# Moving three accumulating weight-sum transfers from a mixer to the feed-forward behind it, and one weight load behind a statistics exchange

## The chip, the cores and the metric

One core of one Trainium2 chip runs the whole program in one launch. The metric is device time in microseconds (us), the median of several runs. Engines are named as in the profile: PE is TensorE, PEld its weight loads, DVE is VectorE, ACT is ScalarE, POOL is GpSimd, SP is SyncE, which here only issues DMAs. An engine's name with a q (SPq) is its queue of instructions.

## The reference

A decoder trunk of two layers on x of shape (1, 512, 1024) in float32. Each layer is a mixer and a gated feed-forward, both between RMS norms and added to the residual:

```
for i in range(2):
    h = rms_norm(x, pre_g);  h = mixer_i(h);  x = x + rms_norm(h, post_g)
    h = conv_ffn(rms_norm(x, ffn_pre_g[i]), w_up[i], conv_w[i], conv_b[i], w_down[i])
    x = x + rms_norm(h, ffn_post_g[i])

def conv_ffn(h, w_up, conv_w, conv_b, w_down):        # 1024 -> 2 x 2816 -> 1024
    u = causal_dwconv(h @ w_up, conv_w, conv_b)       # width 3
    gate, up = split(u, 2);  return (silu(gate) * up) @ w_down
```

The change lies in layer 1. Its mixer projects h to queries, keys and values of three groups of dilated sliding-window attention (group 0 with window 128 and step 1, groups 1 and 2 with steps 4 and 16), whose outputs are merged by the groups' softmax denominators, and of a stick-breaking attention; the concatenated outputs go through one output projection.

## The kernel before, in words

**Products.** Every float32 product is made of three float32r matmuls. A weight block W is loaded raw and split: ACT casts it to a high part (line 84, tile wh), DVE subtracts that to get a low part (line 85, wl). The class `Weights` does this for a list of units in order. `load()` (line 55) takes one of three raw buffers of the tag wraw (128 x 1024) and has SP issue the DMA; `next()` hands out the next split unit and splits ahead by `depth` units. `W` holds nearly all weights of the program; `W2` holds two blocks of the mixer's output weights (od_w_out 0 and 1), split into space that other tiles have left.

**Sums of weights.** The feed-forward's up projection is made, for pairs of blocks 4 to 19, in a scheme of seven block products for eight (Strassen's with Winograd's sums). It needs sums of quarter blocks of the weights. These are not computed by an engine: POOL issues DMAs from DRAM to DRAM, some of which add to their destination (`accum_op`), into four tiles ws per group of pairs ("chunk": three pairs in chunks 0 to 3, two in chunks 4 and 5, as `CHUNKS` says). `sum_steps` (line 148) lists the eight moves of every chunk, step by step and in each step chunk by chunk:

```
steps = [(0, 3, bypass), (2, 2, bypass), (0, 2, add), (2, 0, add), (1, None, bypass),
         (1, 0, add), (3, -1, bypass), (3, 1, add)]          # (tile, source quarter or sum, how)
moves = [lambda c=c, step=step: move(c, *step) for step in steps for c in chunks]
```

The last step adds quarter 1 into tile 3. With a `mark` the list begins with a 4-byte DMA that reads a value of the program, so that the moves start no earlier than that value is there. `make_sums(layer, chunks, mark, left)` issues the moves on POOL but for the last `left`, which it returns.

For layer 1 this happens in three places: chunks 0 to 3 in the mixer from line 1627 (one mark and 32 moves), chunk 4 at the mixer's end (lines 1920, 1931 and 1977) and chunk 5, "its own" (`OWN`), at the begin of the feed-forward (line 405). SP reads the sums as weights (line 60, wraw<-ws), four blocks of 128 x 512 for each pair, the block of tile 3 last, among three blocks that come straight from the input.

**The mixer's end.** The code between line 1878 and line 1945 has its order written out by hand for PE, DVE, ACT, POOL and SP (`manual_schedule`): what stands first is issued first on each engine. A loop of four projections (n = 0 to 3, queries and keys of group 0) goes with the scores and softmaxes of groups 1 and 2 (`score12`, line 1740; `softmax12`, lines 1753 and 1757). `W2.next()` loads and splits od_w_out 0 behind n = 1, and `W2.load()` loads od_w_out 1 behind n = 2. Then:

```
exchange(1, st12)                # SP: write groups 1 and 2's maxima and sums to DRAM (stat)
project = proj_V()               # takes the four split blocks of the values' weights
tile_V(3, "a")                   # PE: values of 128 tokens; ACT copies; SP stores 4 x 64 KB (vst, cv)
exchange_back(1, on)             # SP: read them back in the other order of tokens (on)
for ...: score0(i, banks)        # PE, DVE, ACT: scores and softmaxes of group 0 (lines 1771 to 1780)
exchange(0, st0); tile_V(2, "s"); exchange_back(0, by_r)
W.load(); W.load()
share(st0, on, 0, ...)           # DVE: group 0's share of the merge; needs on (lines 1786 to 1794)
... scale0 (1820); wo2.append(W2.next())   # splits od_w_out 1
```

Then follow two more tiles of values, the other groups' share and scaling (line 1849), the transposes on PE (lines 1830 and 1859), the product with the values (line 1811) and the output projection (tile ao). A DMA that SP may not issue yet, since its buffer or its data aren't there, holds up those behind it on SP.

**The feed-forward's begin.** `ffn` (line 392) has POOL issue a spacer and its own chunk's moves. PE makes four blocks by plain products (u4), then two plain pairs, then the sixteen pairs by seven products (`seven`), whose order is written out by hand for PE, DVE and ACT.

Of the kernel before, what the change touches and what calls it, by code (L numbers as in the profile page):

```python
# [42 lines left out]
OWN = (5,), (5,)  # L43
# [55 lines left out]
def trunk(tc, A, out):  # L99
# [3 lines left out]
    with ExitStack() as top:  # L103
# [7 lines left out]
        def spacer(pool, w):  # L111

            POOL.memset(pool.tile([P, w], F32, tag="spacer", name="spacer", bufs=1)[:, 0:1], 0.0)
# [18 lines left out]
        lead = cst.tile([P, 72], F32, tag="lead", name="lead")  # L132
# [15 lines left out]
        def sum_steps(layer, chunks, mark=None, copies_first=False):  # L148

            wide = "(a q) c -> a (q c)"  # L150
            if layer not in sums_of:
                sums_of[layer] = [[dpool.tile([n * P, S], F32, tag=f"ws{layer}{j}{c}", name="ws")
                                   for c, n in enumerate(CHUNKS[layer])] for j in range(4)]
            tiles = sums_of[layer]

            def move(c, j, src, op):
                if src is None:
                    src = tiles[0][c][:]
                elif src < 0:
                    src = tiles[1][c][:]  # L160
                else:
                    at = sum(CHUNKS[layer][:c]) * P
                    src = A[f"ffn_up_q{layer}"][src, at:at + CHUNKS[layer][c] * P]
                nc.gpsimd.dma_start(tiles[j][c][:].rearrange(wide, q=4), src.rearrange(wide, q=4), accum_op=op,  # L164
                                    max_dma_last_dim=8192)

            steps = [(0, 3, ALU.bypass), (2, 2, ALU.bypass), (0, 2, ALU.add), (2, 0, ALU.add), (1, None, ALU.bypass),
                     (1, 0, ALU.add), (3, -1, ALU.bypass), (3, 1, ALU.add)]
            if copies_first:
                steps[4:] = [(1, 0, ALU.bypass), (3, 1, ALU.bypass), (1, None, ALU.add), (3, -1, ALU.add)]  # L170
            moves = [lambda c=c, step=step: move(c, *step) for step in steps for c in chunks]
            if mark is not None:
                moves.insert(0, lambda: nc.gpsimd.dma_start(tiles[0][chunks[0]][0:1, 0:1], mark))
            return moves

        def make_sums(layer, chunks, mark, left=0):
            moves = sum_steps(layer, chunks, mark)
            with tc.manual_schedule(engines={POOL.engine}):
                while len(moves) > left:
                    moves.pop(0)()  # L180
            return moves
# [20 lines left out]
                    up += [(A["ffn_w_up"][layer, f, z], 1024) for z in range(2)]  # L202
            return (up + [lambda n=n: down[layer](n) for n in range(4 * HF)])

        down, last_rstd = {}, {}
        units = []
        units += [(A["ev_w_c"][u], 832) for u in range(4)]
        units += [(A["ev_w_dqk"][0, 0], 1024), (A["ev_w_dqk"][0, 1], 1024)]
# [183 lines left out]
        def ffn(layer, xnT, pending, final):  # L392
            with ExitStack() as es:
# [8 lines left out]
                                  fp.tile([P, 1024], F32R, tag="gl", name="gl", bufs=HF))  # L402
                with tc.manual_schedule(engines={POOL.engine}):
                    spacer(fp, 80)
                    for move in sum_steps(layer, OWN[layer], last_rstd[layer][0:1, 0:1]) if OWN[layer] else ():
                        move()
                spill = tc_dram[layer]
                t2 = {}
# [1132 lines left out]
        def odd(xnT, pending, order):  # L1541
            xh, xl = xnT
            with ExitStack() as es:
# [44 lines left out]
                def proj_T(*args):  # L1588
                    for _ in T_parts(*args):
                        pass  # L1590
# [33 lines left out]
                DVE.tensor_copy(tri[:], trif[:])  # L1624

                ACT.copy(lead[0:1, 1:2], sv[0:1, 0, 0:1])
                make_sums(1, range(4), lead[0:1, 1:2])


                for u in range(2):  # L1630
# [98 lines left out]
                def score12(hp):  # L1729

                    zps = [[bank(t, "z12", 2, 2, P) for t in tags] for tags in ("ss", "tn")]
                    for rp, zp in enumerate(zps):
                        for rr in range(2):
                            r = 2 * rp + rr
                            c = slice(r * P, (r + 1) * P)
                            for g in range(2):
                                u = 2 * (g + 1) + hp
                                for y in range(2):
                                    rw = slice(y * 64, y * 64 + 64)
                                    PE.matmul(zp[y][:, rr, g], cq[u][rw, c], ck[u][rw, c], start=True, stop=True)  # L1740
                    return [lambda rp=rp, zp=zp: softmax12(hp, rp, zp) for rp, zp in enumerate(zps)]
# [56 lines left out]
                def exchange(n, src):  # L1798

                    d = dpool.tile([S, 8], F32, tag=f"stat{n}", name="stat")  # L1800
                    v = views[n] = [d[:].rearrange("(i q) c -> q i c", i=NT), d[:].rearrange("(q r) c -> q r c", r=4)]
                    nc.sync.dma_start(v[n], src[:].rearrange("p a b c -> p a (b c)"))

                def exchange_back(n, dst):
                    nc.sync.dma_start(dst[:].rearrange("p a b c -> p a (b c)"), views[n][1 - n])
# [68 lines left out]
                W2 = Weights(nc, None, [(A["od_w_out"][k], 1024) for k in range(2)], 2, wpool)  # L1874
# [5 lines left out]
                with tc.manual_schedule(engines={PE.engine, DVE.engine, ACT.engine, POOL.engine, nc.sync.engine}):  # L1880
                    for n, (x, t) in enumerate((x, t) for x in range(2) for t in (cq, ck)):
                        proj_T(t[x], (-0.125, 1.0)[t is ck], False, t is cq)
                        if n % 2 == 0:
                            softmaxes = score12(n // 2)
                        softmaxes.pop(0)()
                        if n == 1:
                            wo2.append(W2.next())
                        if n == 2:
                            W2.load()
                    exchange(1, st12)  # L1890
                    depth, W.depth = W.depth, 0
                    project = proj_V()

                    def tile_V(i, tag):
                        a = project(i, tag=tag)
                        st = chp.tile([P, 512], F32, tag="s", name="vst")
                        ACT.copy(st[:], a)
                        for r in range(4):
                            nc.sync.dma_start(cv12[32 * i:32 * i + 32, r], st[r::4, :])

                    tile_V(3, "a")
                    exchange_back(1, on)
                    for i, banks in zip((3, 2, 1, 0), ("ss", "tn", "aa", "oa")):
                        score0(i, banks)
                    exchange(0, st0)
                    tile_V(2, "s")
                    exchange_back(0, by_r)
                    W.load()
                    W.load()
                    share(st0, on, 0, slice(0, 4))  # L1910
                    for i in ORDER[:2]:
                        scale0(i)
                    wo2.append(W2.next())
                    tile_V(1, "s")
                    for i in ORDER[2:]:
                        scale0(i)
                    share(st12, by_r, 1, slice(0, 4))
                    tile_V(0, "a")

                    moves = sum_steps(1, (4,), shares[1][0:1, 0, 0:1], True)  # L1920
                    halves = [glob.tile([P, 2, 4, 256], F32, tag=tag, name="pt") for tag in ("xh", "xl")]
                    turned_to += [spare[:, 0], spare[:, 1]]
                    turned_to += [sb.tile([P, 4, 256], F32, tag=tag, name="pt")[:] for tag in ("sl", "sh")]
                    turned_to += [x[:, n] for x in halves for n in range(2)]
                    fours = [(hp, rp) for hp in range(2) for rp in range(2)]
                    pts = []
                    for n, i in enumerate(ORDER):
                        pts.append(turn0(i)())
                        scale12(*fours[n])
                        for _ in range((3, 1, 1, 1)[n]):  # L1930
                            moves.pop(0)()
                    for a in fours:
                        pts.append(turn12(*a)())
                    W.ahead(W.pos + 2)
                    oT = [bank("os"[k], "oT") for k in range(2)]
                    oG = [[ap.tile([P, S], F32R, tag=f"{t}{k}", name="og") for k in range(2)] for t in ("cq", "ck")]
                    for u in range(2):
                        for value, pt in zip([value0(i) for i in ORDER] + [value12(*a) for a in fours], pts):
                            value(pt, u)
                        split(oG[0][u][:], oG[1][u][:], oT[u])  # L1940
# [48 lines left out]

        xnT = even()  # L1990
        xnT = ffn(0, *xnT, False)
        xnT = odd(*xnT)
        ffn(1, *xnT, True)


# [99 lines left out]
```

## Time and profile before

| what | value |
|---|---|
| median of 3 runs | 1098.04 us (1097.97 to 1098.35) |
| profiled execution: its time | 1096.47 us |
| profiled execution: its span | 1094.7 us |
| granted PE clock | 0.998 |
| HBM over the span | 258 GB/s |
| POOL's DMA queue (q0) | 9920 packets, 67.12 MB |
| SP's DMA queue (q1) | 61872 packets, 147.73 MB |

The span runs from the first to the last instruction of one profiled execution; the time of that execution has what lies around it too. A row of a timeline has the start in us from the span's start, the duration in us, the engine, the line, the operation, the tile written and the tiles read, how many are merged into the row, and in square brackets how long the engine was idle ahead of it and what ended that. A row of the waits has the sum, the number and the longest. A row of the DMAs has the size of one and the median time from issue to landing in us. A row of a stretch has its length, then for PE, PEld, DVE, ACT and POOL the busy time and the number of instructions, then the granted clock, the share of the DMA engines' time (above 1 when transfers overlap) and GB/s.

### The profile page before, as it was taken

Reading aid. Unit: us, or ns where it says so; the run is one execution under the profiler, and the core shown is the slowest. Engines: PE = TensorE matmul, PEld = TensorE weight load, DVE = VectorE, ACT = ScalarE, POOL = GpSimd, SP = SyncE. Lnnn points to the kernel's source line nnn. Section 1 sums busy time; section 2 is a strip of 40 time slices with the busy share of each in tenths; the row PEclk is TensorE's granted clock in tenths of the full one; section 3 lists DMA queues with packets and bytes.
Section 4 is the critical chain, followed back from the end, with each engine's and each line's share of the span. In section 5 each row is a group of like instructions: output and inputs, shape, how many; then the busy total and the mean of one; then the engine's idle time right before and its main releaser. Section 6 shows DMA issues by size and latency. Waiting matters only on the chain.

```text
span 1094.7 us, 18049 instructions
## 1 busy us (share of the span) xinstructions
PE 1085.6 (99%) x6724; PEld 956.0 (87%) x6724; DVE 907.5 (83%) x1530; ACT 647.8 (59%) x1106; POOL 129.1 (12%) x245
## 2 busy tenths in 40 slices
PE   9999999999999999999999999999999999999997
PEld 8876788898999999888888877889899999988886
DVE  6887786698999999998974775568989999999896
ACT  6565675446666765647553654655656666655561
POOL 3311134220000000000022111124100000000002
PEclk9999999999999999999999999999999999999999
DMA  7797998376565564355618999878845565535452
GB/s 267 257 249 207 259 299 223 104 219 189 174 190 177 176 195 160 125 168 173 245 40 285 274 297 297 231 218 236 234 135 182 174 196 175 188 124 173 153 194 78
DMA packets 72602, 217.26 MB, mean 198 GB/s; under 512 B 10049, under 2 KB 11201, under 8 KB 64321
## 3 DMA queue, kind: packets, MB, share of 16 engines
q1 hardware_dynamic: 61872, 147.73, 40.1%
q0 software_dynamic: 9920, 67.12, 24.5%
q10 hardware_dynamic: 720, 1.25, 0.4%
q8 instruction: 53, 0.87, 0.3%
q14 instruction: 37, 0.30, 0.1%
HBM read 208.69 MB, written 73.43 MB: 258 GB/s over the span
## 4 chain that ended last, share of the span: by engine, by line
PE 97%; DVE 1%; DMA 1%; issue 0%; ACT 0%; SPq 0%; POOLq 0%; DVEq 0%; POOL 0%; ACTq 0%
PE u L327 13%; PE u L326 12%; PE u L325 12%; PE acc L325 6%; PE acc L326 6%; PE acc L327 6%; PE apt L325 3%; PE apt L326 3%; PE apt L327 3%; PE ao L325 2%; PE ao L327 2%; PE ao L326 2%; PE sps L1175 2%; PE aqk L325 1%; PE p L327 1%; PE p L326 1%
## 5 line engine op out<-in xcount | busy, mean ns | idle before, releaser
L85 DVE TENSOR_TENSOR wl<-wraw,wh 128x1024 fp32r<-128x1024 f32 x244 | 295.0, 1216 | 43.2 <-ACT wh L84 42.9
L84 ACT CAST wh<-wraw 128x1024 fp32r<-128x1024 f32 x244 | 251.9, 1046 | 94.7 <-PE u L326 22.8
L327 PE MATMUL u<-xh,wl 128*128 128x256 f32 (+1 forms) x640 | 195.0, 305 | 0.0
L325 PE MATMUL u<-xh,wh 128*128 128x256 f32 (+1 forms) x640 | 195.0, 305 | 0.0
L326 PE MATMUL u<-xl,wh 128*128 128x256 f32 (+1 forms) x640 | 194.8, 304 | 0.0
L327 PEld LDWEIGHTS u<-xh,wl 128*128 128x128 f32 x640 | 122.2, 191 | 5.5 <-DVE wl L85 0.7
L325 PEld LDWEIGHTS u<-xh,wh 128*128 128x128 f32 x640 | 122.2, 191 | 5.0
L326 PEld LDWEIGHTS u<-xl,wh 128*128 128x128 f32 x640 | 122.3, 191 | 5.0
L327 PE MATMUL u<-gh,wl 128*128 128x256 f32 x384 | 108.7, 283 | 0.0
L325 PE MATMUL u<-gh,wh 128*128 128x256 f32 x384 | 108.7, 283 | 0.0
L326 PE MATMUL u<-gl,wh 128*128 128x256 f32 x384 | 108.7, 283 | 0.0
L326 PE MATMUL acc<-wl,gh 128*128 128x512 f32 (+1 forms) x234 | 90.8, 388 | 0.0
L327 PE MATMUL acc<-wh,gl 128*128 128x512 f32 (+1 forms) x234 | 90.6, 387 | 0.0
L325 PE MATMUL acc<-wh,gh 128*128 128x512 f32 (+1 forms) x234 | 90.2, 388 | 0.0
L238 POOL TENSOR_TENSOR rv<-ms,epst 128x1 f32<-128x1 f32 x31 | 13.1, 421 | 629.9 <-ACT junk L292 291.7
L489 ACT ACTIVATE y<-u,cw 128x512 f32<-128x512 f32 x88 | 67.6, 777 | 26.3 <-PE u L327 26.2
L325 PEld LDWEIGHTS u<-gh,wh 128*128 128x128 f32 x384 | 73.7, 192 | 0.1
L326 PEld LDWEIGHTS u<-gl,wh 128*128 128x128 f32 x384 | 73.7, 192 | 0.1
L327 PEld LDWEIGHTS u<-gh,wl 128*128 128x128 f32 x384 | 73.7, 192 | 0.0
L164 POOL DMA_DIRECT2D ws<-in_ffn_up_q x72 | 52.6, 739 | 149.8 <-DMA ws<-ws 74.7
L495 DVE SCALAR_TENSOR_TENSOR y<-u,cw,y 128x510 f32<-128x510 f32 x88 | 65.5, 746 | 2.2
L493 DVE SCALAR_TENSOR_TENSOR y<-u,cw,y 128x511 f32<-128x511 f32 x88 | 65.0, 742 | 2.0 <-ACT y L489 2.0
(400 smaller groups left out, 2478.1 us busy)
## 6 DMA issues: line engine op xcount, KB each, us to landing
ws<-in_ffn_up_q POOLq DMA_DIRECT2D x48, 768.0 KB, 12.5
wraw<-ws SPq DMA_DIRECT2D x128, 256.0 KB, 2.9
wraw<-in_ffn_up_q SPq DMA_DIRECT2D x96, 256.0 KB, 3.0
wraw<-in_ffn_w_down SPq DMA_DIRECT2D x44, 512.0 KB, 3.5
ws<-ws POOLq DMA_DIRECT2D x16, 768.0 KB, 13.1
ws<-in_ffn_up_q POOLq DMA_DIRECT2D x24, 512.0 KB, 6.3
wraw<-in_ffn_w_up SPq DMA_DIRECT2D x24, 512.0 KB, 4.7
wraw<-in_od_w_dqk SPq DMA_DIRECT2D x12, 512.0 KB, 9.7
```

The lines of the kernel that those rows point to most:

```text
L84: self.nc.scalar.copy(h[:, :w], raw[:, :w])
L85: self.nc.vector.tensor_tensor(l[:, :w], raw[:, :w], h[:, :w].bitcast(F32), ALU.subtract)
L164: nc.gpsimd.dma_start(tiles[j][c][:].rearrange(wide, q=4), src.rearrange(wide, q=4), accum_op=op, max_dma_last_dim=8192)
L238: POOL.tensor_tensor(v[:, :n], ms, eps[:, :n], ALU.add)
L325: PE.matmul(o, lh, rh, start=first, stop=False, skip_group_check=more)
L326: PE.matmul(o, lh, rl, start=False, stop=False, skip_group_check=more)
L327: PE.matmul(o, ll, rh, start=False, stop=last, skip_group_check=more)
L489: ACT.activation(y[:, z], u[z], AF.Identity, bias=c[:, 3:4], scale=c[:, 2:3])
L493: DVE.scalar_tensor_tensor(y[:, z, 1:], u[z][:, :S - 1], c[:, 1:2], y[:, z, 1:], ALU.mult, ALU.add)
L495: DVE.scalar_tensor_tensor(y[:, z, 2:], u[z][:, :S - 2], c[:, 0:1], y[:, z, 2:], ALU.mult, ALU.add)
L1175: PE.matmul(ps[z], mq[h][:, i * P:(i + 1) * P], mk[h][:, :w], start=True, stop=True)
```

## The change

The first place in the mixer keeps its last three moves back: step 8 (add quarter 1 into tile 3) of chunks 1, 2 and 3. The feed-forward of layer 1 issues them on POOL behind its mark and ahead of the eight moves of its own chunk. And `W2.load()` leaves the loop (n = 2) and goes behind `exchange_back(1, on)`.

```
-        down, last_rstd = {}, {}
+        down, last_rstd, later_sums = {}, {}, []
...
                     spacer(fp, 80)
-                    for move in sum_steps(layer, OWN[layer], last_rstd[layer][0:1, 0:1]) if OWN[layer] else ():
+                    own = sum_steps(layer, OWN[layer], last_rstd[layer][0:1, 0:1])
+                    if layer:
+                        own[1:1] = later_sums
+                    for move in own:
                         move()
...
                 ACT.copy(lead[0:1, 1:2], sv[0:1, 0, 0:1])
-                make_sums(1, range(4), lead[0:1, 1:2])
+                later_sums.extend(make_sums(1, range(4), lead[0:1, 1:2], 3))
...
                         if n == 1:
                             wo2.append(W2.next())
-                        if n == 2:
-                            W2.load()
                     exchange(1, st12)
...
                     tile_V(3, "a")
                     exchange_back(1, on)
+                    W2.load()
                     for i, banks in zip((3, 2, 1, 0), ("ss", "tn", "aa", "oa")):
                         score0(i, banks)
```

More of the change, by code (lines that the diff above doesn't have):

```diff
@@ L203, in ffn_units @@
             return (up + [lambda n=n: down[layer](n) for n in range(4 * HF)])
-        down, last_rstd = {}, {}
+        down, last_rstd, later_sums = {}, {}, []
         units = []
@@ L404, in ffn @@
                     spacer(fp, 80)
-                    for move in sum_steps(layer, OWN[layer], last_rstd[layer][0:1, 0:1]) if OWN[layer] else ():
+                    own = sum_steps(layer, OWN[layer], last_rstd[layer][0:1, 0:1])
+                    if layer:
+                        own[1:1] = later_sums
+                    for move in own:
                         move()
@@ L1626, in odd @@
                 ACT.copy(lead[0:1, 1:2], sv[0:1, 0, 0:1])
-                make_sums(1, range(4), lead[0:1, 1:2])
+                later_sums.extend(make_sums(1, range(4), lead[0:1, 1:2], 3))
                 for u in range(2):
@@ L1887, in odd @@
                             wo2.append(W2.next())
-                        if n == 2:
-                            W2.load()
                     exchange(1, st12)
@@ L1902, in odd @@
                     exchange_back(1, on)
+                    W2.load()
                     for i, banks in zip((3, 2, 1, 0), ("ss", "tn", "aa", "oa")):
```

## The prediction

> **What bounds the kernel now.** The page comes first: its span, the engines' busy shares, and the chain of work that ended last.
>
> ```profile
> span 1094.7 us, 18049 instructions
> PE 1085.6 (99%) x6724; PEld 956.0 (87%) x6724; DVE 907.5 (83%) x1530; ACT 647.8 (59%) x1106; POOL 129.1 (12%) x245
> PE 97%; DVE 1%; DMA 1%; issue 0%; ACT 0%; SPq 0%; POOLq 0%; DVEq 0%; POOL 0%; ACTq 0%
> ```
>
> The reader sees one engine that ends the program: TensorE is busy 99%, and 97% of the chain is its matmuls. The second view is the busy time by stretches, for the end of layer 0 with the mixer (540 to 760 us) and for the feed-forward behind it.
>
> ```profile
> 540.00:760.00 220.00, 219.94 (x1257) 182.93 (x1256) 143.55 (x298) 119.12 (x222) 48.08 (x80) 1.00 0.82 238
> 760.00:1080.00 320.00, 320.00 (x2114) 295.13 (x2114) 293.20 (x399) 192.91 (x261) 7.61 (x15) 1.00 0.53 168
> ```
>
> The first figure behind the stretch is its length, the second TensorE's busy time. Both stages that the change touches keep TensorE busy to within 0.06 us. Busy can hide short waits, so the third view is the list of waits of the weight loads (PEld), from 180 to 1080 us. In the piece of the mixer that the change touches, two entries are waits for another engine that could be later or earlier:
>
> ```profile
> PEld z L1771 <- DVE st L1753: 0.3, 1, 0.3
> ...
> PEld t L1859 <- ACT spare L1831: 0.3, 1, 0.3
> ```
>
> So 0.6 us is what this execution shows to be won in the mixer. The Trainium skill (Perfetto Trace Analysis, section Identifying the Most-Contended Engine) warns that matmul busy is a poor measure of headroom and points to the weight loads' share instead; by that rule up to 1094.7 - 956.0 = 138.7 us would be open. The list of waits does not bear this out here, but it leaves rival A below its chance.
>
> **The change, part 1: the weight load behind the exchange.** The order on SP's queue, from its timeline:
>
> ```profile
> 675.42 0.33 SPq L62 DMA_DIRECT2D wraw<-in_od_w_out  x1
> 682.59 0.33 SPq L62 DMA_DIRECT2D wraw<-in_od_w_v  x1
> 697.13 0.33 SPq L1802 DMA_DIRECT2D stat<-st  x1
> 697.60 2.46 SPq L1899 DMA_DIRECT2D cv<-vst  x4
> 705.98 0.39 SPq L1805 DMA_DIRECT2D on<-stat  x1
> ```
>
> The row at 675.42 is the load that moves (call it wo-b, 512 KB). It goes behind the read-back at 705.98. Nothing is removed or added: one DMA of 0.33 us on SP passes one weight load (the last of the values', v3), one write of statistics, four stores of values and one read-back. Two things follow.
>
> First, v3 takes the place in the queue, and the raw buffer, that wo-b had: it is issued at about 675.4 instead of 682.59, 7.2 us earlier. Its present cost is here, in the timelines of ACT, DVE and PE:
>
> ```profile
> 691.14 1.05 ACT L84 CAST wh<-wraw 128x1024 fp32r<-128x1024 f32 x1 [1.72 <-DMA wraw<-in_od_w_v]
> ...
> 709.59 1.04 ACT L84 CAST wo<-wraw 128x1024 fp32r<-128x1024 f32 x1
> ```
> ```profile
> 692.23 1.23 DVE L85 TENSOR_TENSOR wl<-wraw,wh 128x1024 fp32r<-128x1024 f32 x1 [3.44 <-ACT wh L84]
> ...
> 708.95 0.18 DVE L1786 TENSOR_TENSOR sm<-st,on 128x16 f32<-128x16 f32 x1 [7.50 <-DMA on<-stat]
> ...
> 712.82 1.21 DVE L85 TENSOR_TENSOR wo<-wraw,wo 128x1024 fp32r<-128x1024 f32 x1
> ```
> ```profile
> 693.82 0.39 PE L326 MATMUL apv<-wl,xh 128*128 128x512 f32 x1
> ```
>
> ACT waits 1.72 us for v3; DVE ends v3's low part at 692.23 + 1.23 = 693.46, and TensorE uses it at 693.82. That is 0.36 us before a stall. With v3 earlier ACT starts up to 1.72 us earlier and the margin grows to about 2 us. DVE's reductions behind it come earlier too, so the 0.3 us wait of the scores (L1771) can go. TensorE itself wins no more than that: it never stood still for v3 in this execution.
>
> Second, wo-b now has a deadline. Its split on DVE stands at 712.82 in a queue that ran without a gap from 708.95, so its cast must end by then, and the load must land by 712.82 - 1.04 = 711.8. It is queued behind the read-back, whose own time depends on the traffic: the answers on DMA for 640 to 700 us and for 700 to 730 us.
>
> ```profile
> wraw<-in_od_w_out SPq DMA_DIRECT2D x2, 512.0 KB, 14.1
> ...
> stat<-st SPq DMA_DIRECT2D x1, 16.0 KB, 8.8
> ```
> ```profile
> wraw<-in_od_w_out SPq DMA_DIRECT2D x2, 512.0 KB, 4.3
> ...
> stat<-st SPq DMA_DIRECT2D x1, 16.0 KB, 2.6
> ```
>
> The same 16 KB write takes 8.8 us beside the sums and 2.6 us without them; the same 512 KB load 14.1 and 4.3 us. So the read-back goes out at the earliest behind the four stores (697.60 + 2.46 = 700.1, later than 697.13 + 2.6), at the latest as now, 706.0. wo-b follows within 0.4 us and lands between 700.5 + 4.3 = 704.8 and 706.4 + 14.1 = 720.5. I take 704.8, because part 2 empties the queue in these microseconds. That is 7 us ahead of the deadline, cost 0. At the other end the price is 720.5 - 711.8 = 8.7 us. Queued behind wo-b on SP are the second statistics write and the stores of values; its raw buffer is free (its three predecessors are split by 693.46), so SP does not stop there.
>
> **Part 2: three sums leave the mixer.** In POOL's timeline the moved DMAs are the last three of this stage:
>
> ```profile
> 688.05 0.80 POOL L164 DMA_DIRECT2D ws<-in_ffn_up_q  x1 [1.82 <-DMA ws<-ws]
> 691.15 0.79 POOL L164 DMA_DIRECT2D ws<-in_ffn_up_q  x1 [2.30 <-DMA ws<-ws]
> 692.73 0.79 POOL L164 DMA_DIRECT2D ws<-in_ffn_up_q  x1 [0.79 <-DMA ws<-ws]
> ```
>
> POOL saves 3 x 0.8 = 2.4 us there and pays it again later; it has no other work at either place. What goes is their traffic across the exchange at 697.13. The read-back then comes up to 706.0 - 700.1 = 5.9 us earlier, and most of DVE's 7.50 us wait at 708.95 goes. DVE and ACT are ahead by so much, and the 0.3 us wait of the transposes (L1859) goes. What is late next? Nothing but TensorE, which has value products to do until it turns the probabilities. Gain 0.3 us, bounds 0 and 0.3.
>
> **Part 3: the same three at the feed-forward's begin.** They come after that stage's marker and before the eight moves of its own group:
>
> ```profile
> 764.09 1.04 POOL L164 DMA_DIRECT2D ws<-in_ffn_up_q  x2 [1.28 <-DMA ws<-rr]
> ```
> ```profile
> 772.12 0.33 SPq L60 DMA_DIRECT2D wraw<-in_ffn_up_q  x1
> 772.54 0.38 SPq L60 DMA_DIRECT2D wraw<-ws  x1
> ...
> 823.59 0.80 SPq L60 DMA_DIRECT2D wraw<-ws  x2
> ```
> ```profile
> 783.70 1.22 DVE L85 TENSOR_TENSOR wl<-wraw,wh 128x1024 fp32r<-128x1024 f32 x1
> ```
> ```profile
> 799.17 0.19 PEld L325 LDWEIGHTS u<-xh,wh 128*128 128x128 f32 x1
> ```
>
> Are the sums in time? Each product pair reads four sum blocks, the moved transfers fill the fourth block of pairs 3 to 11, so the 16th read is the first to need them: the second of the two at 823.59. Issued from 764, and priced like a mixer load of 14.1 us each even one behind the other, they end by 764 + 3 x 14.1 = 806. That is 17 us early, cost 0. The own group follows them by as much and is read by the pairs 14 and 15 alone, later still.
>
> Do they hurt the loads? The first two halves for the seven-product scheme (772.12 and 772.54) must be cast before DVE's split at 783.70, and TensorE needs the result at 799.17. Landing 14.1 us after 772.54, at 786.6, would put the split at 787.7, 4.0 us late, and TensorE would still have it 10 us early. But DVE's queue carries the delay on:
>
> ```profile
> 777.00:799.00 22.00, 22.00 (x102) 18.31 (x101) 21.73 (x29) 16.44 (x20) 2.07 (x3) 1.00 0.80 224
> 799.00:808.00 9.00, 9.00 (x75) 8.92 (x74) 5.89 (x10) 4.06 (x7) 0.00 (x0) 1.00 0.18 60
> ```
>
> The third busy figure is DVE's: 21.73 of 22 us, then 5.89 of 9. The second stretch takes up 3.1 us of 4.0. Cost 0 to 4.0 us; I take 0, since the upper end needs the latency of the mixer's full queue.
>
> **Sum.** -0.3 (scores) - 0.3 (transposes) + 0 + 0 + 0 = -0.6 us. The profiled execution took 1096.47 us (span 1094.7 and 1.8 around it) and would take 1095.9. The median of the runs is 1098.04, 1.57 us above it; the same difference gives **1097.4 us**. No change can be told from noise within 0.2% (2.2 us) here.
>
> **Rivals.**
> A, faster: the timed runs hold stalls that this execution escaped, such as v3's, whose margin was 0.36 us. If all of the 1.57 us is that, the change takes it too: 1098.04 - 1.57 - 0.6 = 1095.9. For it speaks the thin margin; against it that the whole difference would have to sit in this one place.
> B, slower: wo-b late. From 711.8 on, each us goes through the split on DVE to the probabilities and TensorE. Slow by 0.2% from 714.0; at 720.5 it gives 1098.04 + 8.7 = 1106.7. With the early read-back and a full-queue load, 700.5 + 14.1 = 714.6, it gives 1100.8. For it speaks that such loads did take 14.1 us; against it that the sums then beside them are gone.
> C, slower: the feed-forward's loads stand behind the three sums, as the 16 KB write did (8.8 against 2.6 us). DVE is 4.0 us late and recovers nothing: 1102.0. For it speaks DVE's 21.73 of 22; against it TensorE's 15 us between split and use. The Trainium skill (DMA: Bandwidth & Descriptors, section Queues, rings and completion order) states that a DMA engine serves its queues in turn, a whole packet of typically 9 to 17 descriptors at a time, so that a small transfer waits out a neighbour's packet; the two rows of the 16 KB write agree with it, and it is what speaks most against part 3.
> D, the forecast itself in other words: both waits are hidden work and nothing changes, 1098.0.
>
> **Chances.** Forecast and D 0.80, A 0.10, B 0.06, C 0.04. A ends at the border of 0.2%, so half of it counts as faster: faster 0.05, same 0.85, slower 0.10. The range runs from A's 1095.8 to a mild B or C, 1100.2; the likeliest case alone is 1097.2 to 1098.3.
>
> **What would show it.** Right: v3's load near 675, wo-b's behind the read-back, the read-back near 700, DVE's wait for it under 2 us, the two 0.3 us waits gone, TensorE 99% busy, no SP wait for a sum after 800. Wrong: a wait of ACT for wo-b and a gap on TensorE near 718 (B); ACT waiting for loads from 772 on and gaps on TensorE between 790 and 815 (C); a wait elsewhere, from an order of loads or splits that the compiler's scheduling changed with the edit.

## The result, and the profile after

| kernel | median | runs |
|---|---|---|
| before | 1098.52 us (1096.84 to 1100.33) | 14 |
| after | 1096.28 us (1095.91 to 1097.08) | 14 |

The ratio is 0.998, with a 95% interval of 0.9972 to 0.9988: 2.2 us faster (1.3 to 3.1). The interval leaves out 1, but the size lies just at the 0.2% below which the prediction calls nothing a change, and by that border it counts as the same. The runs also lie closer together: their spread falls from 3.5 to 1.2 us. The profiled execution took 1096.35 us. That is only 0.12 us less than the one the prediction was made from, because 1096.47 us was lower than every one of the 14 runs of before. Most of the story lies in that.

The page of after, its span, the engines and the chain of work that ended last:

```profile
span 1094.5 us, 18048 instructions
PE 1085.0 (99%) x6724; PEld 956.1 (87%) x6724; DVE 907.8 (83%) x1530; ACT 647.4 (59%) x1106; POOL 127.2 (12%) x245
PE 98%; DVE 1%; issue 0%; ACT 0%; POOLq 0%; DVEq 0%; POOL 0%; ACTq 0%
```

The two stretches, in the same columns as before:

```profile
540.00:760.00 220.00, 219.98 (x1264) 183.63 (x1264) 144.34 (x298) 120.13 (x223) 44.30 (x77) 1.00 0.77 228
760.00:1080.00 320.00, 320.00 (x2111) 294.93 (x2110) 293.06 (x399) 192.22 (x261) 10.12 (x18) 1.00 0.57 175
```

The traffic has moved (DMA share 0.82 to 0.77 and 0.53 to 0.57), and TensorE's busy time in the feed-forward is still the whole stretch. SP's queue, then ACT's casts of v3 and of wo-b, then DVE's first step on the read-back:

```profile
695.14 0.33 SPq L1805 DMA_DIRECT2D stat<-st  x1
695.84 3.22 SPq L1900 DMA_DIRECT2D cv<-vst  x4
699.16 0.53 SPq L1808 DMA_DIRECT2D on<-stat  x1
699.73 0.50 SPq L62 DMA_DIRECT2D wraw<-in_od_w_out  x1
```
```profile
689.17 1.03 ACT L84 CAST wh<-wraw 128x1024 fp32r<-128x1024 f32 x1
...
704.82 1.03 ACT L84 CAST wo<-wraw 128x1024 fp32r<-128x1024 f32 x1
```
```profile
701.39 0.17 DVE L1789 TENSOR_TENSOR sm<-st,on 128x16 f32<-128x16 f32 x1
```

Neither cast waits for its load now (v3's waited 1.72 us), the read-back goes out at 699.16 instead of 705.98, and DVE takes it up without a wait (it waited 7.50 us). The whole list of waits of the weight loads from 685 to 760 us is down to three short ones without another engine in them:

```profile
PEld z L1774 <- issue: 0.4, 1, 0.4
PEld ao L325 <- issue: 0.2, 1, 0.2
PEld oT L1814 <- issue: 0.2, 1, 0.2
```

A clock for the mixer's end is the start of the first product with the values, behind the transposes. Its row in the timeline of TensorE, before and after:

```profile
722.41 1.09 PE L1811 MATMUL oT<-spare,cv 128*64 128x128 f32 x16
```
```profile
721.46 1.09 PE L1814 MATMUL oT<-spare,cv 128*64 128x128 f32 x16
```

So even in the lucky execution of before TensorE was 0.95 us late there. Of this, 0.60 us came at the scores and 0.42 at the transposes (its value products had begun 0.07 us earlier than after). Busy time had shown 0.06 of it: the 32 matmuls of the scores stand in the timeline as 3.91 us before and 3.31 after, both without a gap, although their weight loads waited.

### The profile page after: what moved, and what is told of

Read it like the earlier page. It is cut to its first block, busy times and chain, and to the rows that moved or that the text cites. A ratio compares the mean times of both kernels' runs of the same rounds, so it can differ in the third digit from the quotient of the medians.

```text
span 1094.5 us, 18048 instructions
## 1 busy us (share of the span) xinstructions
PE 1085.0 (99%) x6724; PEld 956.1 (87%) x6724; DVE 907.8 (83%) x1530; ACT 647.4 (59%) x1106; POOL 127.2 (12%) x245
## 4 chain that ended last, share of the span: by engine, by line
PE 98%; DVE 1%; issue 0%; ACT 0%; POOLq 0%; DVEq 0%; POOL 0%; ACTq 0%
PE u L327 13%; PE u L325 12%; PE u L326 12%; PE acc L325 6%; PE acc L326 6%; PE acc L327 6%; PE apt L325 3%; PE apt L326 3%; PE apt L327 3%; PE ao L325 2%; PE ao L327 2%; PE ao L326 2%; PE sps L1178 2%; PE aqk L325 1%; PE p L327 1%; PE p L326 1%
```

## The experiments

wo-b and v3 are as in the prediction. Three theories went in. V: v3 is late in most executions of before. X: the exchange is late, its write held up beside the sums. Z: it lies elsewhere, at the program's start or tail. Kernels of one group ran on one chip with 33 to 35 (the last group 21) runs of the kernel before.

**The parts alone** (before 1098.86 us). The kernel before again:

> The kernel before, unchanged, for a second profiled execution and more times. Its 14 times run from 1096.84 to 1100.33 us, those of the changed kernel from 1095.91 to 1097.08. Theory V (the last value weights, v3, land too late in most executions; margin 0.36 us in the profile of before): a gap on TensorE near 693.8 us, and the scores behind it late by the same. Theory X (the exchange's 16 KB write through the sums' traffic takes longer in most executions than the 8.8 us shown): the wait of DVE at line 1786 longer than 7.5 us and a gap on TensorE at the transposes near 716 to 722 us. Theory Z (the place is elsewhere, the start or the output's last DMA): TensorE's matmuls from 600 to 760 us as in the first profile, and the difference ahead of them or behind the last. Median expected 1098.0 to 1098.8.

The sums moved, the load left in the loop:

```
                         if n == 1:
                             wo2.append(W2.next())
+                        if n == 2:
+                            W2.load()
...
                     exchange_back(1, on)
-                    W2.load()
```

> The three sums go to the feed-forward's begin, the weight load stays in the loop. Theory X: the exchange is free of the sums' traffic, all of the gain is here, 1096.2 to 1096.6. Theory V: v3 is still issued second, at about 682.6 us, with the same sums ahead of it as before the moved ones start; half the gain or less, 1097.3 to 1098.3. Theory Z: as the kernel before, 1098.0 to 1098.8, or no relation.

The load moved, the sums left in the mixer (the kernel before with the last two hunks of the change):

> The weight load goes behind the exchange's read-back, the three sums stay in the mixer. Theory V: v3 is issued near 675 us, all of the gain, 1096.2 to 1096.8. Theory X: the 16 KB write still passes through the sums, now with the weight load landing after it as well; no gain, 1098.0 to 1100, and the split of the late load may wait on top.

As the sums alone, but the three sums are never issued (three quarter sums of the second layer lack their last addend):

```
-                        own[1:1] = later_sums
+                        pass
```

> As the run with the sums alone, but the three moved transfers are never issued, neither in the mixer nor in the feed-forward, so three of the sums lack one addend and the output is another. It prices the third part: if the transfers at the feed-forward's begin cost nothing, its time is that of the run with the sums alone within 0.4 us; if they cost what rival C says, it is up to 4 us faster.

| kernel | median us | ratio to before, 95% |
|---|---|---|
| before again | 1097.8 | 0.9994 (0.9985 to 1.0002) |
| sums alone | 1097.0 | 0.9987 (0.9978 to 0.9996) |
| load alone | 1097.61 | 0.9991 (0.9982 to 1.0) |
| sums left out | 1097.1 | 0.9986 (0.9977 to 0.9995) |

Leaving the sums out is worth no more than moving them (1097.1 and 1097.0). The runs resolve about 1 us either way; the profiles are finer: from the first product with the values to the last matmul it is 365.30 us with the sums alone and 365.31 with the sums left out. At the feed-forward's begin the three cost nothing. By the ratios the sums alone save 1.4 us (0.4 to 2.4) and the load alone 1.0 (0 to 2.0). Both medians lie between what V and X expected, and the unedited kernel, 0.06% below itself, shows how little 11 runs can resolve. The profile of this second execution of before (1099.59 us), the three longest waits of the weight loads from 685 to 760 us:

```profile
PEld apv L326 <- DVE wl L85: 1.1, 1, 1.1
PEld apv L325 <- ACT wh L84: 0.6, 1, 0.6
PEld z L1771 <- DVE st L1753: 0.5, 1, 0.5
```

TensorE does stand still for v3, for its cast (wh) and its low part (wl); the prediction's execution had escaped it. With the sums alone the wait is smaller, not gone (the two longest):

```profile
PEld apv L326 <- DVE wl L85: 0.5, 1, 0.5
PEld z L1774 <- DVE st L1756: 0.5, 1, 0.5
```

With the load alone both are gone and no wait in this list is longer than 0.4 us; wo-b's cast waits 1.36 us for its load, and no wait of TensorE is listed for it.

**V against X** (before 1098.21 us). The changed kernel again, and two that put wo-b just ahead of the statistics write, where v3 and wo-b have merely changed places: one with the sums moved, one with the sums as before.

```
+                    W2.load()
                     exchange(1, st12)
...
                     exchange_back(1, on)
-                    W2.load()
```

> The changed kernel unedited. Theory S (the two parts save separately: the early v3 about 1.0 us, as the load alone did, 1098.86 to 1097.61 with 0.2 of drift; the sums out of the exchange about 1.4 us, as the sums alone did): 2.2 to 2.6 us below the kernel before. Theory O (one stall, of which each part alone takes the same share): no more than either alone, 1.2 to 1.8 us below.

> The changed kernel with wo-b issued just ahead of the statistics write instead of behind the read-back, so that v3 and wo-b have only changed places. If v3's place is what counts: as the changed kernel, within 0.3 us; v3's cast waits for nothing, wo-b is issued near 682.5. If wo-b must be behind the exchange: as with the sums alone, 0.6 to 1.0 us above the changed kernel, and DVE's wait for the read-back is longer than in the changed kernel.

> The kernel before with v3 and wo-b changed in place, the sums untouched. If v3's place is what counts: as with the load alone behind the read-back, about 1.0 us below the kernel before, and the cast of wo-b does not wait (with the load behind the read-back it waited 1.36 us). If it is the load's place behind the exchange: as the kernel before, within 0.3 us.

And six moves at the feed-forward's begin instead of three:

```
-                later_sums.extend(make_sums(1, range(4), lead[0:1, 1:2], 3))
+                later = sum_steps(1, range(4), lead[0:1, 1:2])
+                with tc.manual_schedule(engines={POOL.engine}):
+                    for n in (*range(26), 29):
+                        later[n]()
+                later_sums.extend(later[n] for n in (26, 30, 27, 31, 28, 32))
```

> The changed kernel with six moves instead of three issued at the feed-forward's begin: the copies of quarter 3 (step 7) and the additions of quarter 1 (step 8) of chunks 1, 2 and 3, ordered by chunk. If the sums' traffic ahead of the exchange still costs (v2's cast waited 2.51 us for its load in the changed kernel): 0.3 to 1.0 us below the changed kernel. If the stalls are gone with three: within 0.3 us of it. If the feed-forward's begin has no more room: slower, the first late read being that of chunk 1's fourth block near 823.

| kernel | median us | ratio to before, 95% |
|---|---|---|
| after again | 1096.18 | 0.9981 (0.9973 to 0.999) |
| swap and sums | 1096.08 | 0.9981 (0.9973 to 0.999) |
| swap alone | 1098.54 | 1.0 (0.9991 to 1.0008) |
| six moves | 1097.68 | 1.0002 (0.9991 to 1.0013) |

The changed kernel again is 2.1 us below before by its ratio, between theories S and O. With the sums moved, it is worth nothing that wo-b goes behind the exchange: swap and sums does as well. But the swap alone, which brings v3 as early as the change does, saves nothing that these runs show, against V in its plain form. (The load alone had 0.9991, and the two intervals overlap: whether wo-b's place counts while the sums are in the mixer stays open.) The longest wait of the weight loads in the profile of the swap alone:

```profile
PEld t L1830 <- ACT vst L1896: 1.0, 1, 1.0
```

v3's and the scores' waits for another engine are gone, and one that was in no earlier list stands at the transposes. Since this execution took 1097.07 us, near the lowest of its kernel, it was profiled once more:

> The kernel with v3 and wo-b changed in place and the three sums untouched, once more for a profile (its first profile, 1097.07 us, was near the lowest of its eleven times, median 1098.54). If its time is lost at the transposes, which stand behind the exchange: no wait for v3 and none of the scores, the statistics' write 9 us or more, and TensorE's waits at the transposes between 716 and 720 us explain what it has above 1096.2 us (except a wait near 150 us). If the early v3 does not hold: waits for v3's split near 693 again.

It took 1098.21 us. DVE's first step on the read-back, then ACT, then TensorE, from the timelines:

```profile
710.61 0.17 DVE L1786 TENSOR_TENSOR sm<-st,on 128x16 f32<-128x16 f32 x1 [9.77 <-DMA on<-stat]
```
```profile
717.95 0.23 ACT L1789 ACTIVATE sm<-sm 128x32 f32<-128x32 f32 x1 [5.19 <-DVE sm L1788]
718.16 0.58 ACT L1896 COPY vst<-apv 128x512 f32<-128x512 f32 x1
718.65 2.06 ACT L1831 COPY spare<-t 128x512 f32<-128x512 f32 x4
```
```profile
714.29 2.44 PE L1830 MATMUL t<-ident,s 128*128 128x128 f32 x20
718.80 1.42 PE L1830 MATMUL t<-ident,s 128*128 128x128 f32 x8 [2.07 <-ACT vst L1896]
```

Read upwards: TensorE has done 20 of 28 transpositions and waits 2.07 us for ACT to empty a bank. ACT is held by its own order: the exponentials of the second share (L1789) stand ahead of the copy of the last value tile, and they wait 5.19 us for DVE, which had waited 9.77 us with the first share because the read-back was late. Not only the write is slow in the two profiles of the swap alone (9.2 and 10.0 us), the read-back behind it is too: 4.5 and 5.0 us to landing, where the prediction's execution had 2.9. In the second profile of the changed kernel the same two rows of ACT are these:

```profile
711.42 0.23 ACT L1792 ACTIVATE sm<-sm 128x32 f32<-128x32 f32 x1 [1.33 <-DVE sm L1791]
714.94 0.59 ACT L1898 COPY vst<-apv 128x512 f32<-128x512 f32 x1 [3.29 <-PE apv L327]
```

There the copy waits for TensorE and not TensorE for the copy, with 3.3 us to spare. So V and X both hold, one behind the other: a TensorE that is late for v3 meets an exchange that is late anyway, and what the swap alone wins at the first it loses at the second.

Six moves lose at the other end, in the feed-forward. In the profile (1100.56 us, the second slowest of 12 runs) ACT's cast waits for a sum block, and TensorE's weight load for the cast:

```profile
818.79 1.05 ACT L84 CAST wh<-wraw 128x1024 fp32r<-128x1024 f32 x1 [4.53 <-DMA wraw<-ws]
```
```profile
821.55 0.19 PEld L325 LDWEIGHTS u<-gh,wh 128*128 128x128 f32 x1 [2.54 <-ACT wh L84]
```

This is not chunk 1's fourth block, as was expected: counted as in the prediction, the blocks of chunk 1 are read from 821 us on only. From 806 to 820 us the loads of sums land in 5.5 us (median), against 3.6 in the changed kernel.

**How many sums** (before 1098.17 us). The third argument of the first place is 1, then 2, instead of 3; and the kernel before once more.

```
-                later_sums.extend(make_sums(1, range(4), lead[0:1, 1:2], 3))
+                later_sums.extend(make_sums(1, range(4), lead[0:1, 1:2], 1))
```

> The changed kernel with one sum moved instead of three: the additions of quarter 1 into chunks 1 and 2 stay in the mixer. Theory X (each sum in flight when the 16 KB of statistics are written makes the write longer; 8.7 to 9.5 us with three such sums in four profiles, 2.4 to 3.5 with none in the mixer's last 8 us): the write takes 5 to 7.5 us, the transposes wait 0 to 0.5 us, 1096.4 to 1097.4 us. Rival T (any sum there does the whole damage): 8.5 us or more, 1097.6 to 1098.5, as the swap alone.

> The changed kernel with two sums moved: the addition into chunk 1 stays in the mixer, issued near 689. Theory X: the write takes 2.5 to 5 us, no wait of the transposes, 1096.1 to 1096.6 us, the changed kernel's 1096.2 within 0.4. Rival T: 7 us or more and over 1097.

> The kernel before, unedited, for one more profile. If its spread (1095.96 to 1100.38 us) comes from the mixer's end: TensorE waits there, at the values of v3, the scores or the transposes, explain what this execution has above 1096.2 us, except for a wait near 150 us in the other layer (0.9 to 2.3 us, seen in three of ten profiles).

One moved sum: 1096.11 us, 0.9982 (0.9973 to 0.9991). Two: 1096.25 us, 0.9984 (0.9976 to 0.9993). Both do all that three do. The statistics' write in the DMA answers for 676 to 700 us, with one sum moved and then with two:

```profile
stat<-st SPq DMA_DIRECT2D x1, 16.0 KB, 8.6
```
```profile
stat<-st SPq DMA_DIRECT2D x1, 16.0 KB, 5.0
```

With one moved the write is as slow as in the kernel before, as rival T said, and the time is not, against T and below X's range. With two, the write and the time are what X expected. The rows of the kernel with one moved show why it loses nothing:

```profile
705.07 0.17 DVE L1789 TENSOR_TENSOR sm<-st,on 128x16 f32<-128x16 f32 x1 [3.79 <-DMA on<-stat]
```
```profile
708.16 1.05 ACT L84 CAST wo<-wraw 128x1024 fp32r<-128x1024 f32 x1 [2.36 <-DMA wraw<-in_od_w_out]
```

The write began at 694.32 (697.13 in the prediction's execution, 695.46 with the swap profiled last), the first share comes at 705.07 and not at 710.61, and the slack of 3.3 us takes up the rest: DVE and ACT wait, TensorE does not. Within these kernels it is a matter of slack and not of the write's length alone. None of them beats the change by more than the runs can tell.

The third profile of before (1098.03 us), the five longest waits from 685 to 760 us:

```profile
PEld apv L326 <- DVE wl L85: 1.1, 1, 1.1
PEld apv L325 <- ACT wh L84: 0.5, 1, 0.5
PEld z L1771 <- DVE st L1753: 0.5, 1, 0.5
PEld z L1771 <- issue: 0.4, 1, 0.4
PEld t L1859 <- ACT spare L1831: 0.3, 1, 0.3
```

So two profiles of before out of three hold v3's stall. This one has no long wait near 150 us, so the whole excess can be read here. Five starts on TensorE in this profile, then in the second of after (1096.14 us): the first value product, the scores, the next value product, the first transposition, the first product with the values.

```profile
689.30 0.39 PE L325 MATMUL apv<-wh,xh 128*128 128x512 f32 x1
696.27 4.09 PE L1771 MATMUL z<-ck,cq 64*128 64x256 f32 x32
700.29 0.50 PE L325 MATMUL apv<-wh,xh 128*128 128x512 f32 x1
716.77 3.33 PE L1830 MATMUL t<-ident,s 128*128 128x128 f32 x28
723.96 1.09 PE L1811 MATMUL oT<-spare,cv 128*64 128x128 f32 x16
```
```profile
689.48 0.39 PE L325 MATMUL apv<-wh,xh 128*128 128x512 f32 x1
695.01 3.31 PE L1774 MATMUL z<-ck,cq 64*128 64x256 f32 x32
698.24 0.50 PE L325 MATMUL apv<-wh,xh 128*128 128x512 f32 x1
714.70 3.22 PE L1833 MATMUL t<-ident,s 128*128 128x128 f32 x28
721.34 1.09 PE L1814 MATMUL oT<-spare,cv 128*64 128x128 f32 x16
```

Up to the scores 6.97 us against 5.53 (v3's stall: 1.44 us), up to the next value product 4.02 against 3.23 (the scores: 0.79), from the first transposition to the first product with the values 7.19 against 6.64 (the transposes: 0.55). At the end 723.96 stands against 721.34: 2.62 us lost at the mixer's end. The two times differ by 1.89. The rest went at the tail. The last matmul, in this profile of before (span 1096.3) and then in the second of after (span 1094.3):

```profile
1089.19 0.28 PE L327 MATMUL acc<-wh,gl 128*128 128x256 f32 x1
```
```profile
1086.64 0.28 PE L327 MATMUL acc<-wh,gl 128*128 128x256 f32 x1
```

From its start to the span's end it is 7.1 us there and 7.7 here: the change gives back 0.6 us, and 2.62 - 0.6 = 2.0 against 1.89 measured. The last output store lands 2.0 us after its issue in the one and 2.7 in the other. This goes by kernel: the tail is 7.0 to 7.1 us in the five profiles of before and of the swap alone, and 7.5 to 8.0 in the nine of all other kernels, the load alone (2.8 for the store) among them. The store does not explain all of it (2.0 us with the sums left out, whose tail is 7.5). Why was not tried and stays open.

The same three stretches in all profiles, the start of the first product with the values, and the time of the same execution, in us:

| profile | value products | scores | transposes | first product with the values | time |
|---|---|---|---|---|---|
| before, the prediction's | 5.54 | 3.84 | 7.06 | 722.41 | 1096.47 |
| before, the second | 7.07 | 4.02 | 7.44 | 725.51 | 1099.59 |
| before, the third | 6.97 | 4.02 | 7.19 | 723.96 | 1098.03 |
| load alone | 5.53 | 3.24 | 7.29 | 723.27 | 1098.71 |
| swap alone, the two | 5.53, 5.53 | 3.24, 3.24 | 8.36, 9.79 | 723.01, 724.08 | 1097.07, 1098.21 |
| sums alone | 5.91 | 4.03 | 6.65 | 722.33 | 1097.0 |
| sums left out | 5.72 | 4.01 | 6.64 | 722.21 | 1096.78 |
| after, after again | 5.53, 5.53 | 3.24, 3.23 | 6.64, 6.64 | 721.46, 721.34 | 1096.35, 1096.14 |
| swap and sums | 5.53 | 3.24 | 6.64 | 723.52 | 1098.25 |
| one sum, two sums | 5.53, 5.53 | 3.24, 3.23 | 6.64, 6.64 | 721.38, 721.26 | 1096.06, 1095.93 |
| six moves | 5.53 | 3.23 | 6.64 | 721.84 | 1100.56 |

725.51, 723.27 and 723.52 have 0.9, 1.2 and 2.3 us from the wait near 150 us in them. The first two stretches go by v3's place: wherever v3 comes early they are 5.53 and 3.23 to 3.24 us, with the sums moved or not; elsewhere they are 5.54 to 7.07 and 3.84 to 4.03. The third goes by the sums: 6.64 or 6.65 us wherever at least one of the three is out of the mixer, 7.06 to 9.79 with all three in it. So each part of the change mends a stretch of its own. The sums help v3 as well: its load, issued at 682.4 to 683.6 us where it stands second, landed in 8.5 us in the prediction's execution, in 10.2 in both others of before, and in 9.1 and 8.9 with the sums alone and with the sums left out. Behind this point the kernels hardly differ: to the last matmul it is 365.2 to 365.3 us, but for the load alone (365.9) and six moves (368.9). So within the kernel before the time follows this start (374.1 us lie behind it in all three executions), and theory Z is left with the wait near 150 us and the tail.

## Why the prediction was right or wrong

The forecast was 1097.4 us in a range of 1095.8 to 1100.2. The measured 1096.28 lies inside it, 1.1 us below the forecast and near its lower end, but below the 1097.2 to 1098.3 given for the likeliest case alone. By the border of 0.2% it counts as the same, which had a chance of 0.85; "faster" had 0.05. The effect was -0.6 us by the sum and -2.2 measured: the direction was right, the size was not. What came nearest was rival A's 1095.9, which had 0.10; without A the range would have missed.

- **The step that failed** is in part 1: "TensorE itself wins no more than that: it never stood still for v3". That was true of one execution with a margin of 0.36 us, in a queue whose landings move by more than that: v3's load took 8.5 us there and 10.2 in the two other profiles of before. In these the weight loads wait 1.1 us for v3's low part and 0.5 to 0.6 for its cast, and TensorE loses 1.4 and 1.5 us up to the scores. The term for v3 was 0 and should have been about 1.4 us in such an execution. After the change the low part is ready at 691.47 and used at 693.90, a margin of 2.4 us, as predicted.
- **The scores' term** (-0.3) was mis-sized: the wait in the list was 0.3 us, but the stretch is 0.60 us longer than after in the prediction's own execution and 0.8 in the other two.
- **The transposes' term** (-0.3, bounds 0 and 0.3) was somewhat small (0.42, 0.55 and 0.80 us in the three profiles of before), and the upper bound was wrong. It left out that v3 and the exchange cover for each other: with v3 early and the sums left in, the stretch is 0.65 us (load alone) and 1.7 and 3.2 us (swap alone) longer. "What is late next? Nothing but TensorE" was asked of the whole change only, where it holds.
- **The tail** is in no term: it takes back about 0.6 us, and this stays unexplained. That A's figure is off by only 0.4 us is in part luck: terms that were too small stand against a tail that was left out.
- **Rival A** named the mechanism; what was held against it, that all of it would have to sit in one place, was no objection. In the third profile of before the excess does sit at the mixer's end, between 693 and 724 us.
- **wo-b's deadline** (part 1): it was issued at 699.73 where 700.1 was worked out, and its cast did not wait. Cost 0 as predicted. The deadline's working says that DVE's queue ran without a gap from 708.95; it had one of 0.29 us, at 709.71, which changes nothing here. Rival B did not come: even with two of the three sums still in the mixer, where ACT waited 2.36 us for this load, the cast came at 708.16, ahead of the deadline of 711.8. It was nearest with the load alone, where the cast came at 711.89 in an execution that ran 1.2 us late from 150 us on.
- **Part 2**: the read-back went out at 699.16 (predicted 700.1), and DVE's wait went from 7.50 us to none listed.
- **Part 3**: cost 0 as predicted, shown by the sums left out. The loads there did slow down; the DMA answers for 762 to 800 us, before and then after:

```profile
wraw<-ws SPq DMA_DIRECT2D x8, 256.0 KB, 3.5
wraw<-in_ffn_up_q SPq DMA_DIRECT2D x6, 256.0 KB, 4.8
```
```profile
wraw<-ws SPq DMA_DIRECT2D x8, 256.0 KB, 5.4
wraw<-in_ffn_up_q SPq DMA_DIRECT2D x6, 256.0 KB, 6.7
```

Two microseconds each, under the 15 us between split and use: rival C's price was not reached. Six moves show the limit of that cover: 1097.68 us, a ratio to before of 1.0002, and so the gain of the mixer lost again.
- **The base.** The 1.57 us between the profiled execution and the median was carried over unchanged, as if it were something common to both kernels. In the third profile of before, whose 1098.03 us are near that median, the first product with the values starts 1.55 us later than in the first, and the time is 1.56 us longer: there the difference is v3's stall (1.43 us) and more of the waits behind it, which the change removes. How often the stall comes, three profiles cannot say.

The Trainium skill (Perfetto Trace Analysis, section Identifying the Most-Contended Engine) holds matmul busy for a poor measure of headroom. Here the trace agrees in the small: 219.94 us busy of 220.00 stood beside 0.95 us lost. The weight loads' share of 87% did not show it either, being 87% before and after; only the start times did.

## What to carry to other kernels

A margin of a few tenths of a microsecond behind a DMA is a toss of a coin, not a margin: when the profiled execution is well below the median of the runs, look in it for the waits that just did not happen, and take a second profile before pricing one at nothing. Two late things in a row on one path hide each other, so price each with the other mended; a part tried alone can show nothing and still be needed for the gain. And compare the start of the same instruction in two profiles rather than busy time.

## What the runs showed of the hardware

- The same 16 KB write took 8.7 to 10.0 us beside the three sums (in all six profiles of kernels that issue them in the mixer), 8.6 with one of them gone, 5.0 with two gone (one profile each) and 2.4 to 2.8 with all three gone (six profiles): not an equal step per transfer. The Trainium skill (DMA: Bandwidth & Descriptors, section Queues, rings and completion order) says that a DMA engine goes round the queues that have work, a packet at a time; a write that waits out packets of a busy neighbour agrees with that, but no run here shows the packets themselves.
- A wait in the other layer, near 150 us, is 0.9 to 2.3 us longer than its usual 0.4 in three of the fourteen profiles (before again, load alone, swap and sums), with the change and without it; it is a part of the spread that no edit here touched.
